# Transposed tiles of a hybrid RWKV-7/HGRN2 layer, moved as 1 KB or 384 B pieces and ordered by a ScalarE copy

## The chip, the core and the metric

The kernel runs on one core of a Trainium2 chip. The core has a matrix engine (TensorE, PE in the profile), whose weight loads are listed apart as PEld, three engines for element work (VectorE or DVE, ScalarE or ACT, GpSimd or POOL), a sync engine (SyncE or SP) that here issues nearly all DMAs, and 16 DMA engines. Each engine works through its own list of instructions in order and waits on semaphores of the others. The metric is device microseconds for one execution of the whole layer, the median of several.

## What is computed

One layer over 512 frames of 2048 channels. A combined input projection feeds two mixers of 1024 channels each. The first is RWKV-7 with 16 heads of 64 channels, the second HGRN2 with 8 heads of 128. Their gated outputs go through one output projection, a residual sum and a layer norm.

```python
# RWKV-7, per head, per frame t
sa = einsum('bhij,bhj->bhi', S, a_t)
S = S * w_t + sa[..., None] * b_t + v_t[..., None] * k_t
o_t = einsum('bhij,bhj->bhi', S, r_t)
...
# HGRN2, per head, chunk by chunk
k_dec = k_c * exp(b_last - b)
S = S * exp(b_last)[..., None] + einsum('bshd,bshv->bhdv', k_dec, i_c)
o = einsum('btsh,bshv->bthv', att, i_c) + einsum('bthd,bhdv->bthv', q_c * exp(b), S)
...
y = concat([o_rwkv * silu(z_r), norm(o_hgrn) * silu(z_h)]) @ W_out
h = layer_norm(ALPHA * h + y)
```

## The kernel before

**The projections.** All projection matmuls are made of three products of split operands: a tile is split into a rounded part (`xh`, `wh`) and the rest (`xl`, `wl`), both in a reduced fp32 format, and `three` (L457) adds hi*hi, hi*lo and lo*hi. A unit of 128 output channels takes 16 channel tiles of the input, so 48 matmuls of 128x512 in one bank of PSUM. The first three units are made by another loop (L1205). Weights arrive as `wr` tiles by DMA; ScalarE makes `wh` (L342), VectorE makes `wl` (L352). The units follow one another in the order of `_order`: for each group of two RWKV channel pairs p the keys k, r and v, the gates z of the group before, then q, f, i and g of the HGRN heads. PSUM has 8 banks, 4 called `main` (projection units and some mixer products) and 4 called `mix`.

**The mixers.** Their work runs beside the projections. RWKV is prepared pair by pair (`rwkv_prep`), then two pairs make a group (`rwkv_group`): a triangular inverse, `folded`, a serial scan over 8 chunks of 64 frames (`rwkv_scan`), `outputs` and `rwkv_finish`. HGRN heads go in twos through `hgrn_heads` and then one by one through `hgrn_out`. In the profile, L329 is a mixer matmul, L333 a transpose by TensorE, L342 and L343 ScalarE activations, L352 a VectorE tensor_tensor, L361 a scalar_tensor_tensor (it also evacuates a projection unit, `t<-main,pr,t`), L371 the VectorE transpose of 32x32 blocks, L310 a DMA that SyncE issues.

**What sets the order.** The kernel is written out instruction by instruction by a planner (`Plan`) that keeps an estimated clock for each engine. Each projection matmul is followed by `pump`, which lets the waiting threads (generators) issue what can start now by those clocks. So the cost that a thread's operation is given decides where everything behind it lands in all engines' lists; on the chip the lists are fixed, and only semaphores hold an engine. The planner knows three kinds of TensorE work (`main`, `whole`, `narrow`), with a cost for each change between them. It puts off mixer matmuls until some are together.

**Buffers.** A thread takes a tile when its pool (`BUFS`) has a free slot by the planner's account and drops it after its last use. A projection unit's bank is emptied into a `t` tile, of which there are 18. When they are short, units wait in their banks (`evac_room`).

**The transposes in question.** Three kinds of tile are transposed with channels and frames changing places: `bk` (beta and k of RWKV, 128x1024 for one pair), v (128x512, written to rows 64 to 127 of the tile `zz`), and k of HGRN heads 0 to 5 (128x384, the first three tiles of 128 frames). VectorE transposes 32x32 blocks (`dtr`) into a `tmp` tile; the blocks then have to change places across partitions, which DMAs do (`turned`): for each of 4x4 (or 4x2) pairs of blocks one DMA of 32 partitions. In each partition such a DMA moves 8 (or 3) runs of 32 floats, 128 B each, straight to the places where matmuls read them. Heads 6 and 7 use TensorE instead.

Of the kernel before, what the change touches and what calls it, by code (L numbers as in the profile page):

```python
# [15 lines left out]
P = 128  # L16
# [225 lines left out]
def mixer_kernel(ctx, tc, head, x_r, w_all, par, up, ln_wb, consts, hmask, out):  # L242
# [127 lines left out]
    def dtr(o, i):  # L370
        return dve_op([i], o, lambda: dve.transpose(o, i), per=0.0019)  # L371
# [22 lines left out]
            f = lambda: dve.tensor_copy(o, i)  # L394
        return Op([act_way(o, i, AF.Copy, scale), ("dve", 0.075 + size(o) * 0.00105 + moved(o, i), f)], [i], [o])

    def turned(dst, src, tmp, rows=4, base=0):


        name = dst.tensor.name  # L400
        yield dtr(tmp, src)
        yield lambda: by_now(tmp)
        for a in range(4):
            for b in range(rows):
                yield lambda: plan.clock["sp"] <= plan.clock["pe"] + 0.2
                o = base + 32 * b
                send(dst[o : o + 32, :, 32 * a : 32 * a + 32],
                     tmp[32 * a : 32 * a + 32, :, 32 * b : 32 * b + 32], 0.65)
        plan.ready[name] = plan.busy[tmp.tensor.name] = (plan.clock["sp"] + 2.6, "dma")

# [213 lines left out]
            ups.append(upw)  # L624

    hc = [slice(64 * h, 64 * h + 64) for h in range(2)]

    def rwkv_prep(S, p):
        if p == 0:
# [71 lines left out]
        drop(pf)  # L701
        yield stt(r, r, hcol(HRK, p), k, ALU.mult, ALU.mult)
        drop(k)
        S["ar"], S["bk"] = ar, bk

        odd = p % 2
        if odd == 0:
# [16 lines left out]

        yield room(q4=1)
        tmp = take("q4", [P, NCH, P])
        yield from turned(bk, bk, tmp)
        drop(tmp)
        yield has(S, "v")
        yield room(ksq=2)  # L730
        rh, rl = (take("ksq", [P, T], F32R) for _ in range(2))
# [9 lines left out]
        S["bv"] = r  # L741

        yield room(zz=1)
        z = take("zz", [P, NCH, P])
        yield room(ksq=1)
        tmp = take("ksq")
        yield from turned(z, chunks(v), chunks(tmp), rows=2, base=64)
        drop(v, tmp)
        S["zz"] = z

    def folded(SS, sc):

        yield lambda: all("zz" in S for S in SS)
        zs, bks = ([S[n] for S in SS] for n in ("zz", "bk"))
        yield room(main=2, mix=2)
        yield landed(*zs, *bks, sc)
        pvs = [take("main") for _ in SS]
        pbs = [take("mix") for _ in SS]
        for half, (z, bk, pv, pb) in enumerate(zip(zs, bks, pvs, pbs)):
            for c in range(NCH):  # L760
                i, cs = half * 16 + 2 * c, slice(c * C, c * C + C)
                for h in range(2):
                    yield mm(pv[hc[h], cs], sc[64:128, 0, i + h], z[64:128, c, hc[h]])
                    yield mm(pb[hc[1 - h], cs], sc[0:64, 0, i + 1 - h], bk[0:64, c, hc[1 - h]])
        more = plan.free("mix", 2)
        prs = []

        def beside():
            prs.extend(take("mix") for _ in SS)
            for half, pr_ in enumerate(prs):  # L770
                for c in range(NCH):
                    for h in range(2):
                        i = half * 16 + 2 * c + h
                        yield mm(pr_[hc[h], c * C : c * C + C], sc[0:64, 0, i], sc[0:64, 1, i])

        if more:
            yield from beside()
        for pv, z, pb, bk in zip(pvs, zs, pbs, bks):
            for h in range(2):
                yield copy(bk[0:64, :, hc[h]], chunks(pb[hc[h]]))  # L780
                yield copy(z[0:64, :, hc[h]], chunks(pv[hc[h]]), scale=-1.0)
# [12 lines left out]
        yield from keep()  # L794

    def outputs(SS, sc):

        yield room(mix=2)
        pss = [take("mix") for _ in SS]
        for half, (S, po) in enumerate(zip(SS, pss)):  # L800
            z = S["zz"]
            yield lambda z=z: by_now(z)
            for c in range(0, NCH, 2):
                for h in range(2):
                    for e in range(2):
                        yield mm(po[hc[e], c // 2 * P + 64 * h : c // 2 * P + 64 * h + 64],
                                 sc[:, 1, half * 16 + 2 * (c + e) + h], z[:, c + e, hc[h]])
# [45 lines left out]
    def rwkv_scan(SS, sc):  # L853
# [15 lines left out]
        olds = [None] * 2  # L869
        for c in range(NCH):  # L870
            more = c < NCH - 1
            zs = [zz[:, c] for zz in zzs]
            news = [bds[c % 2] for bds in bdss]
            pxs = []
            if c > 0:
                yield landed(*olds)
                yield room(mix=2)
                for ar, old in zip(ars, olds):
                    pxs.append(take("mix"))
                    yield mm(pxs[-1][:, :P], ar[:, c], old)  # L880
                for px, z in zip(pxs, zs):
                    yield tt(z[0:64], z[0:64], px[0:64, :P], ALU.subtract)
# [181 lines left out]
    def hgrn_out(S, h, q, k, dt_, dg, tot, tots):  # L1064

        yield room(g=1)
        g = take("g")
        kt, state = tiles(g)[:, 0:3], tiles(k)[:, 0:3]
        if h < 6:
            yield room(ksq=1)  # L1070
            tmp = take("ksq")
            yield from turned(kt, tiles(k)[:, 0:3], tiles(tmp)[:, 0:3])
            drop(tmp)
        else:
            yield landed(k)
# [6 lines left out]
        yield room(rs=1)  # L1082
        i_all = S["i"]
        hs = slice(h % 4 * P, h % 4 * P + P)
        yield landed(i_all, g)
        ps = take("mix")
        for t in range(3):
            yield mm(ps[:, t * P : t * P + P], kt[:, t], i_all[:, t, hs])
# [591 lines left out]
```

## Time and profile before

| what | us |
|---|---|
| median of 3 runs (lowest, highest) | 1052.14 (1050.43, 1052.18) |
| the profiled execution | 1049.71 |
| its span, first to last instruction | 1047.9 |
| ScalarE busy in the span | 436.8 |
| VectorE busy in the span | 754.5 |
| GpSimd busy in the span | 41.8 |

The granted TensorE clock was 0.999 over the span. The profiled execution took 1.8 us more than its span. An instruction's row gives its start, its busy time and, in brackets, the idle time of its engine before it and what ended that. TensorE matmuls are pipelined: their busy times overlap and their ends are modelled, so what a matmul costs is read from one start to the next. "main<-xh,wh" reads: bank `main`, written from tiles `xh` and `wh`.

### The profile page before, as it was taken

The numbers are of one execution on the slowest core, as the hardware profiler recorded it, in microseconds if no ns is written. First come the engines' busy times: TensorE is split into PE (matmuls) and PEld (weight loads), VectorE is DVE, ScalarE is ACT, GpSimd is POOL, SyncE is SP. The second block draws the span as 40 slices with busy tenths as digits, with TensorE's granted clock in tenths as the row PEclk, the third lists the DMA queues.
The fourth block names the chain that finished last, engine by engine and source line by source line (L and its number), as shares of the span: only waits on it lengthen the run. The fifth ranks groups of instructions, "written<-read, shape, count | busy, mean of one in ns | idle before, by whom it ended". The sixth has DMA issues, their size and how long they took to land.

```text
span 1047.9 us, 19640 instructions
## 1 busy us (share of the span) xinstructions
PE 1034.7 (99%) x7708; PEld 857.5 (82%) x7708; DVE 754.5 (72%) x1599; ACT 436.8 (42%) x817; POOL 41.8 (4%) x77
## 2 busy tenths in 40 slices
PE   9999999999999999999999999999999999999997
PEld 7888888888888888878888788888888888888885
DVE  7474898767759988667689767775999886526456
ACT  6444434543443355353533364435335444223321
POOL 0000001001000010010000100100001011000000
PEclk9999999999999999999999999999999999999999
DMA  9135342133253432224443222344342245445613
GB/s 332 53 103 130 90 104 85 60 93 99 77 140 94 123 87 68 87 74 113 112 116 104 82 73 73 105 110 106 105 117 81 64 157 183 145 129 170 193 60 131
DMA packets 98061, 116.03 MB, mean 111 GB/s; under 512 B 67120, under 2 KB 68912, under 8 KB 97840
## 3 DMA queue, kind: packets, MB, share of 16 engines
q1 hardware_dynamic: 97824, 114.57, 37.1%
q8 instruction: 61, 1.00, 0.4%
q14 instruction: 32, 0.26, 0.1%
q10 hardware_dynamic: 144, 0.20, 0.1%
HBM read 99.92 MB, written 7.34 MB: 102 GB/s over the span
## 4 chain that ended last, share of the span: by engine, by line
PE 93%; DMA 2%; DVE 2%; SPq 1%; issue 1%; ACT 0%; POOL 0%; DVEq 0%
PE main L457 70%; PE mix L329 11%; PE mix L457 8%; PE main L1205 3%; DMA wr<-w_all 2%; PE main L329 1%; PE mix L333 1%; SPq L310 1%; DMA q<-head 0%; DVE t L352 0%; DVE wl L352 0%; DVE inv L361 0%; DMA g<-ksq 0%; ACT t L342 0%; DVE q L361 0%
## 5 line engine op out<-in xcount | busy, mean ns | idle before, releaser
L457 PE MATMUL main<-xh,wh 128*128 128x512 f32 x864 | 339.6, 393 | 1.9 <-DVE t L361 1.9
L457 PE MATMUL main<-xh,wl 128*128 128x512 f32 x864 | 341.2, 395 | 0.0
L457 PE MATMUL main<-xl,wh 128*128 128x512 f32 x864 | 339.7, 393 | 0.0
L342 ACT ACTIVATE wh<-wr 128x512 fp32r<-128x512 f32 x299 | 186.5, 627 | 244.7 <-PE main L457 193.6
L352 DVE TENSOR_TENSOR wl<-wr,wh 128x512 fp32r<-128x512 f32 x299 | 203.3, 682 | 75.1 <-ACT wh L342 73.6
L457 PEld LDWEIGHTS main<-xh,wh 128*128 128x128 f32 x864 | 162.4, 188 | 35.3 <-DVE t L361 2.3
L457 PEld LDWEIGHTS main<-xh,wl 128*128 128x128 f32 x864 | 162.4, 188 | 33.3 <-DVE wl L352 0.3
L457 PEld LDWEIGHTS main<-xl,wh 128*128 128x128 f32 x864 | 162.3, 188 | 33.2
L457 PE MATMUL main<-wl,xh 128*128 128x512 f32 (+1 forms) x262 | 102.2, 390 | 0.3 <-DVE wl L352 0.3
L457 PE MATMUL main<-wh,xh 128*128 128x512 f32 (+1 forms) x262 | 102.1, 390 | 0.0
L457 PE MATMUL main<-wh,xl 128*128 128x512 f32 (+1 forms) x262 | 101.8, 388 | 0.0
L457 PEld LDWEIGHTS main<-wl,xh 128*128 128x128 f32 x262 | 49.2, 188 | 10.3 <-DVE wl L352 0.6
L457 PEld LDWEIGHTS main<-wh,xh 128*128 128x128 f32 x262 | 49.2, 188 | 10.2 <-ACT wh L342 0.2
L457 PEld LDWEIGHTS main<-wh,xl 128*128 128x128 f32 x262 | 49.2, 188 | 9.8
L361 DVE SCALAR_TENSOR_TENSOR bd<-mix,pc,bd 64x64 f32<-64x64 f32 x112 | 31.7, 283 | 17.1 <-PE mix L329 15.0
L343 ACT ACTIVATE t<-main,om 128x512 f32<-128x512 f32 x33 | 22.2, 686 | 51.6 <-PE main L457 42.4
L342 ACT ACTIVATE t<-mix 64x128 f32<-64x128 f32 (+2 forms) x65 | 17.6, 272 | 56.6 <-PE mix L329 28.2
L352 DVE TENSOR_TENSOR inv<-inv 64x30 f32<-64x30 f32 (+14 forms) x120 | 38.5, 321 | 2.8
L352 DVE TENSOR_TENSOR inv<-inv,inv 64x30 f32<-64x30 f32 (+14 forms) x120 | 38.5, 321 | 2.7
L361 DVE SCALAR_TENSOR_TENSOR t<-main,pr,t 128x511 f32<-128x511 f32 x33 | 24.3, 745 | 19.7 <-ACT t L343 19.6
L352 DVE TENSOR_TENSOR t<-t,tot 128x256 f32<-128x256 f32 x96 | 37.5, 417 | 0.3
L343 ACT ACTIVATE t<-main 128x512 f32<-128x512 f32 x32 | 18.6, 595 | 32.5 <-PE main L457 32.3
(218 smaller groups left out, 1311.9 us busy)
## 6 DMA issues: line engine op xcount, KB each, us to landing
wr<-w_all SPq DMA_DIRECT2D x156, 512.0 KB, 3.7
q<-head SPq DMA_DIRECT2D x15, 448.0 KB, 6.1
q<-q SPq DMA_DIRECT2D x128, 32.0 KB, 2.7
g<-x_r SPq DMA_DIRECT2D x16, 256.0 KB, 4.0
spill<-g SPq DMA_DIRECT2D x12, 256.0 KB, 3.7
t<-spill SPq DMA_DIRECT2D x12, 256.0 KB, 4.3
out<-q SPq DMA_DIRECT2D x12, 256.0 KB, 2.5
zz<-ksq SPq DMA_DIRECT2D x64, 32.0 KB, 3.0
```

The costliest lines, as they stand in the source:

```text
L310: nc.sync.dma_start(o, i)
L329: return Op([("pe", cost, lambda: pe.matmul(o, l, r, start=start, stop=stop, **kw))], [l, r], [o], mode="narrow" if narrow else "main" if ...
L333: return Op([("pe", 0.11, lambda: pe.transpose(o, i, ident))], [i], [o])
L342: return "act", cost, lambda: sc_e.activation(o, i, f, scale=scale)
L343: return "act", cost, lambda: sc_e.activation(o, i, f, scale=scale, bias=bias)
L352: return dve_op([a, b], o, lambda: dve.tensor_tensor(o, a, b, f), base=0.16 if o.shape[0] < P and size(o) == C and o.tensor.name in tags e ...
L361: return dve_op([a, b], o, lambda: dve.scalar_tensor_tensor(o, a, s, b, f1, f2), per=0.00113, base=0.085 if o.shape[0] == P else 0.25 if s ...
L457: pe.matmul(ps, l, r, start=first and i == 0, stop=last and i == 2)
L1205: pe.matmul(pss[a], *ops, start=k == 0 and low == of == 0, stop=k == KT - 1 and low == 1)
```

## The change

The DMAs of `turned` stay as many as before, and each moves as many bytes. But now the block transpose of VectorE writes its blocks so that what one DMA moves lies together in each partition (`tmp` is indexed block row first, then chunk). The DMA writes to a place where it lies together too: one run of 1 KB (384 B for HGRN keys) in each of 32 partitions. The destination of the DMAs is the source tile itself for `bk` and v, and the head's `g` tile for HGRN keys. A ScalarE copy then puts the blocks into order: `bk` into `tmp`, which takes the name `bk` from there on (8 copies of 128x1024); v into rows 64 to 127 of `zz` (two copies of 64x512 for each of 8 pairs); HGRN keys from `g` back into the k tile (6 copies of 128x384). `zz` is now laid out as four blocks of 32 channels, each with all 8 chunks, so the matmuls that read one chunk of it take two or four runs of 32 floats at a stride of 1 KB, and the VectorE operations that write it do likewise. The planner is told 0.5 us for the issue of one piece, before 0.65 us.

```diff
-    def turned(dst, src, tmp, rows=4, base=0):
-        name = dst.tensor.name
-        yield dtr(tmp, src)
+    def blocks(t, n):
+        return t.rearrange("p (a c j) -> p a c j", a=4, c=n)
+
+    def turned(dst, src, tmp, rows=4):
+        yield dtr(tmp.rearrange("p b c j -> p c b j"), src)
         yield lambda: by_now(tmp)
         for a in range(4):
             for b in range(rows):
                 yield lambda: plan.clock["sp"] <= plan.clock["pe"] + 0.2
-                o = base + 32 * b
-                send(dst[o : o + 32, :, 32 * a : 32 * a + 32],
-                     tmp[32 * a : 32 * a + 32, :, 32 * b : 32 * b + 32], 0.65)
-        plan.ready[name] = plan.busy[tmp.tensor.name] = (plan.clock["sp"] + 2.6, "dma")
+                o = dst(a, b)
+                send(o, tmp[32 * a : 32 * a + 32, b], 0.5)
+        plan.ready[o.tensor.name] = plan.busy[tmp.tensor.name] = (plan.clock["sp"] + 2.6, "dma")
...
         tmp = take("q4", [P, NCH, P])
-        yield from turned(bk, bk, tmp)
-        drop(tmp)
+        bk4 = blocks(bk.rearrange("p c f -> p (c f)"), NCH)
+        yield from turned(lambda a, b: bk4[32 * b : 32 * b + 32, a], bk, blocks(tmp.rearrange("p c f -> p (c f)"), NCH))
+        yield act(tmp.rearrange("p c (a j) -> p c a j", j=32), bk4.rearrange("p a c j -> p c a j"), AF.Copy)
+        drop(bk)
+        S["bk"] = tmp
...
-        z = take("zz", [P, NCH, P])
+        z = take("zz", [P, 4, NCH, 32])
         yield room(ksq=1)
-        tmp = take("ksq")
-        yield from turned(z, chunks(v), chunks(tmp), rows=2, base=64)
-        drop(v, tmp)
+        tmp = take("ksq", [P, 2, NCH, 32])
+        v4 = v.rearrange("p (a c j) -> p a c j", a=2, c=NCH)
+        yield from turned(lambda a, b: v4[64 * (a // 2) + 32 * b : 64 * (a // 2) + 32 * b + 32, a % 2],
+                          chunks(v), tmp, rows=2)
+        drop(tmp)
+        for h in range(2):
+            yield act(z[64:128, hb[h]], v4[hc[h]], AF.Copy)
+        drop(v)
...
-                    yield mm(pv[hc[h], cs], sc[64:128, 0, i + h], z[64:128, c, hc[h]])
+                    yield mm(pv[hc[h], cs], sc[64:128, 0, i + h], z[64:128, hb[h], c])
...
-            zs = [zz[:, c] for zz in zzs]
+            zs = [zz[:, :, c] for zz in zzs]
...
-        kt, state = tiles(g)[:, 0:3], tiles(k)[:, 0:3]
+        kt = state = tiles(k)[:, 0:3]
         if h < 6:
             yield room(ksq=1)
             tmp = take("ksq")
-            yield from turned(kt, tiles(k)[:, 0:3], tiles(tmp)[:, 0:3])
+            g4 = blocks(g[:, : 3 * P], 3)
+            yield from turned(lambda a, b: g4[32 * b : 32 * b + 32, a], kt, blocks(tmp[:, : 3 * P], 3))
             drop(tmp)
+            yield act(kt.rearrange("p c (a j) -> p c a j", j=32), g4.rearrange("p a c j -> p c a j"), AF.Copy)
...
-        yield landed(i_all, g)
+        yield landed(i_all, k)
```

Since the planner's clocks change, the lists of all engines change too. TensorE has the same matmuls as before, in 135 stretches of mixer work between projection matmuls where there were 138. Three places matter below; the number behind a tile's name only tells tiles apart.

The first place is TensorE's list around the output of HGRN head 2 (`mix_4825` before, `mix_4822` now) and the border between two projection units, the gate z of pair 2 (`main_4752`, now `main_4773`) and the key of pair 5 (`main_4866`, now `main_4891`). Before, the border comes 11 projection matmuls behind the head's last product:

```order
L329 MATMUL mix_4825<-t_3494,t_3389 128x128
L457 MATMUL main_4752<-xl_96,wh_4786 128x512
L457 MATMUL main_4752<-xh_80,wl_4787 128x512
...
L457 MATMUL main_4752<-xl_99,wh_4786 128x512
L457 MATMUL main_4752<-xh_83,wl_4787 128x512
L457 MATMUL main_4866<-xh_68,wh_4816 128x512
```

Now it comes 24 projection matmuls and the head's four TensorE transposes behind it:

```order
L329 MATMUL mix_4822<-t_3511,t_3399 128x128
L459 MATMUL main_4773<-xh_76,wh_4786 128x512
L459 MATMUL main_4773<-xl_92,wh_4786 128x512
...
L459 MATMUL main_4773<-xh_82,wl_4787 128x512
L333 MATMUL mix_4868<-cst,t_3399 128x128 x4
L459 MATMUL main_4773<-xh_83,wh_4813 128x512
L459 MATMUL main_4773<-xl_99,wh_4813 128x512
L459 MATMUL main_4773<-xh_83,wl_4814 128x512
L459 MATMUL main_4891<-xh_68,wh_4845 128x512
```

The head's output moved ahead by 13 projection matmuls against the unit border.

The second place is VectorE's list there, where the head's scaled output (`t<-mix,rs`) and the evacuation of the key of pair 4 (`main_4212`, now `main_4234`) stand. Before:

```order
L365 TENSOR_REDUCE rs_4837<-t_3389 128x4
L358 TENSOR_SCALAR rs_4837<-rs_4837 128x4
L352 TENSOR_TENSOR wl_4846<-wr_4703,wh_4845 128x512
L352 TENSOR_TENSOR t_3389<-mix_4825,rs_4837 128x512
L361 SCALAR_TENSOR_TENSOR t_4859<-main_4212,pr,t_4859 128x511
```

Now:

```order
L365 TENSOR_REDUCE rs_4835<-t_3399 128x4
L358 TENSOR_SCALAR rs_4835<-rs_4835 128x4
L352 TENSOR_TENSOR wl_4846<-wr_4769,wh_4845 128x512
L352 TENSOR_TENSOR t_3399<-mix_4822,rs_4835 128x512
L361 SCALAR_TENSOR_TENSOR t_4856<-main_4234,pr,t_4856 128x511
```

Here nothing moved: the evacuation still stands directly behind the head's scaled output.

The third place is ScalarE's list at HGRN head 0, where one of the new copies stands. Now:

```order
L342 ACTIVATE wh_2399<-wr_2288 128x512
L342 ACTIVATE t_1047<-g_2263 128x384
L342 ACTIVATE wh_2419<-wr_2288 128x512
L342 ACTIVATE t_1047<-mix_2432 128x128
L342 ACTIVATE bd_2118<-bd_2119,pc_627 128x128
```

The copy `t_1047<-g_2263` is new; behind it on ScalarE stand a weight split, the head's first state (which before stood there without the copy), and a decay of the scan's state.

More of the change, by code (lines that the diff above doesn't have):

```diff
@@ L626, in mixer_kernel, with halves @@
     hc = [slice(64 * h, 64 * h + 64) for h in range(2)]
+    hb = [slice(2 * h, 2 * h + 2) for h in range(2)]
+    def halves(t):
+        return t.rearrange("p (c a j) -> p c a j", a=2, j=32)
     def rwkv_prep(S, p):
@@ L703, in rwkv_prep @@
         drop(k)
-        S["ar"], S["bk"] = ar, bk
+        S["ar"] = ar
         odd = p % 2
@@ L780, in folded @@
                 yield copy(bk[0:64, :, hc[h]], chunks(pb[hc[h]]))
-                yield copy(z[0:64, :, hc[h]], chunks(pv[hc[h]]), scale=-1.0)
+                yield copy(z[0:64, hb[h]].rearrange("p a c j -> p c a j"), halves(pv[hc[h]]), scale=-1.0)
             drop(pv, pb)
@@ L806, in outputs @@
                         yield mm(po[hc[e], c // 2 * P + 64 * h : c // 2 * P + 64 * h + 64],
-                                 sc[:, 1, half * 16 + 2 * (c + e) + h], z[:, c + e, hc[h]])
+                                 sc[:, 1, half * 16 + 2 * (c + e) + h], z[:, hb[h], c + e])
         for S, po in zip(SS, pss):
@@ L881, in rwkv_scan @@
                 for px, z in zip(pxs, zs):
-                    yield tt(z[0:64], z[0:64], px[0:64, :P], ALU.subtract)
+                    yield tt(z[0:64], z[0:64], px[0:64, :P].rearrange("p (a j) -> p a j", j=32), ALU.subtract)
                 if more:
```

## The prediction

> **What bounds the kernel now.** I read the page's first table, then who TensorE (PE) waited for, then the timeline at each of those waits.
>
> ```profile
> span 1047.9 us, 19640 instructions
> PE 1034.7 (99%) x7708; PEld 857.5 (82%) x7708; DVE 754.5 (72%) x1599; ACT 436.8 (42%) x817; POOL 41.8 (4%) x77
> ```
>
> TensorE is busy in 99% of the span; ScalarE (ACT) and VectorE (DVE) are not. So a transfer or a copy can change the time only where TensorE stands still for it, or where the change gives TensorE more or slower work. All its waits fit in seven lines (total us, times, longest):
>
> ```profile
> PE main L457 <- DVE t L361: 1.9, 1, 1.9
> PE mix L329 <- ACT ksq L1422: 1.5, 1, 1.5
> PE mix L329 <- issue: 1.3, 3, 0.8
> PE main L329 <- issue: 1.3, 1, 1.3
> PE mix L1155 <- DVE inv L1153: 1.1, 1, 1.1
> PE mix L329 <- DMA g<-ksq: 0.6, 1, 0.6
> PE main L457 <- DVE wl L352: 0.3, 1, 0.3
> ```
>
> They add up to 8.0 us, 0.8% of the span: no removal of waits can bring more. Only one of them, `g<-ksq`, is a wait for a DMA that the change touches. The waits on ksq L1422 and inv L1153 are at the end and the start of the kernel, where nothing changes. What the change does to the other lines it does by moving work.
>
> **The largest wait, for a bank.** First TensorE, then VectorE, at 455 to 460 us; the columns are start, busy time, instruction.
>
> ```profile
> 455.13 0.39 PE L329 MATMUL mix<-t,t 128*128 128x128 f32 x2
> 455.27 0.48 PE L457 MATMUL main<-xl,wh 128*128 128x512 f32 x1
> 457.44 0.39 PE L457 MATMUL main<-xl,wh 128*128 128x512 f32 x1
> 457.68 0.39 PE L457 MATMUL main<-xh,wl 128*128 128x512 f32 x1
> 459.98 0.50 PE L457 MATMUL main<-xh,wh 128*128 128x512 f32 x1 [1.92 <-DVE t L361]
> ...
> 456.19 0.69 DVE L365 TENSOR_REDUCE rs<-t 128x4 f32<-128x512 f32 x1 [2.12 <-ACT t L343]
> 458.58 0.69 DVE L352 TENSOR_TENSOR t<-mix,rs 128x512 f32<-128x512 f32 x1 [0.90 <-POOL rs L384]
> 459.19 0.74 DVE L361 SCALAR_TENSOR_TENSOR t<-main,pr,t 128x511 f32<-128x511 f32 x1
> ```
>
> Projection matmuls start 0.23 us apart (457.44 to 457.68); here one starts 2.30 us after the one before, so 2.07 us are lost. The key of pair 5 needs the bank of the key of pair 4, four units older, whose evacuation ends at 459.19 + 0.74 = 459.93. That evacuation stands behind HGRN head 2 on VectorE: reduce, GpSimd's reciprocal root, scaled output. The head's last product starts at 455.13, so the bank comes free 4.80 us after it. TensorE has only 11 projection matmuls to fill this, and arrives at 459.98 - 2.07 = 457.91.
>
> **Part 1: the order.** The rows of TensorE's order say that 24 projection matmuls and four transposes now lie in this place, while VectorE's rows keep the evacuation directly behind the head. Twenty-four steps of 0.23 us are 5.5 us, more than the 4.80 us that the bank takes. The wait should go: **-2.07 us**, and 0.7 us plus the transposes remain as a margin. What is late next there: the transposes need the scaled output, which ends at 458.58 + 0.69 = 459.27, 4.14 us behind the last product, and they stand 21 steps, 4.8 us, behind it. That fits by 0.7 us. Bounds: 0 to -2.07.
>
> **Part 2: the pieces.** The wait of `g<-ksq` is at HGRN head 0:
>
> ```profile
> 257.39 0.39 PE L457 MATMUL main<-xl,wh 128*128 128x512 f32 x1
> 258.33 0.91 PE L329 MATMUL mix<-ia,g 128*128 128x128 f32 x6 [0.56 <-DMA g<-ksq]
> ...
> 253.16 1.87 SPq L310 DMA_DIRECT2D g<-ksq  x3
> ...
> q<-q SPq DMA_DIRECT2D x128, 32.0 KB, 2.7
> zz<-ksq SPq DMA_DIRECT2D x64, 32.0 KB, 3.0
> g<-ksq SPq DMA_DIRECT2D x96, 12.0 KB, 2.2
> out<-inv SPq DMA_DIRECT2D x2, 128.0 KB, 3.1
> ```
>
> The product starts 0.94 us after the matmul before it where 0.23 is usual: 0.71 us lost. Three pieces took 1.87 us of the sync engine's time, 0.62 each, and the last was issued at about 254.4. The planner counted 0.65 a piece and now counts 0.5. What a piece of 32 runs takes there isn't in the trace; the nearest row is the weight load of 128 partitions, 0.33:
>
> ```profile
> 256.92 0.33 SPq L310 DMA_DIRECT2D wr<-w_all  x1
> ```
>
> Between 0.33 and 0.62 I take 0.33, since a new piece has fewer runs than that load. Sixteen pieces are then done 16 x (0.5 - 0.33) = 2.7 us before the planner counts on them, where before the gain was 16 x (0.65 - 0.62) = 0.5 us. This wait should go: **-0.71 us**, bounds 0 to -0.71.
>
> How soon a piece lands would matter as well. Pieces in runs of 128 B land in 2.2 to 3.0 us, a store of 128 KB in long rows in 3.1: short runs cost little here. The Trainium skill, "DMA: Bandwidth & Descriptors", section "Why small descriptors are slow (HBM only)", says that transfers within SBUF don't suffer from small descriptors as those to HBM do; the rows agree. It speaks against this part: if transport is all that the change shortens, the 0.71 us stay and the sum below ends 0.7 us higher. I keep the term, because it comes from the issue, 0.62 us a piece, and not from the landing.
>
> **Part 3: the added copies.** No row shows them; these are the nearest:
>
> ```profile
> L342 ACT ACTIVATE wh<-wr 128x512 fp32r<-128x512 f32 x299 | 186.5, 627 | 244.7 <-PE main L457 193.6 <-PE mix L457 32.9 <-DMA wr<-w_all 6.9
> L342 ACT ACTIVATE q<-mix 64x512 f32<-64x512 f32 x16 | 9.5, 593 | 8.1 <-PE mix L329 8.0
> L342 ACT ACTIVATE t<-q 128x384 fp32r<-128x384 f32 x15 | 7.6, 510 | 1.4 <-DMA q<-head 1.4
> ```
>
> Eight copies of 1024 at twice 0.63 are 10.1 us, 16 of 64x512 at 0.59 are 9.5, 6 of 384 at 0.51 are 3.1: **22.7 us** on ScalarE, whose 436.8 us busy leave 611 us idle. As work they lie beside TensorE and cost nothing; the cover is that ScalarE's splits (`wh`) run ahead until a buffer holds them, as their 193.6 us of waiting for projection matmuls show. The price is the new wait: each copy waits on ScalarE for DMA pieces, and behind it in the list stand weight splits and evacuations, as in the third place of the order. VectorE needs `wh` for `wl`, TensorE needs both, and the sync engine's next weight load waits for `wl`. If a copy waits longer than the splits are ahead, TensorE stands. Bounds: 0, and 22 groups (8 `bk`, 8 v, 6 k) each late by as much as the one wait on pieces above, 22 x 0.71 = 15.6 us. Since one group in 22 was late before, I take one again: **+0.7 us**. So parts 2 and 3 cancel; they are kept apart because they can fail apart.
>
> **Part 4: the rest of TensorE's work.** The matmuls are the same. Three fewer returns from mixer work to projections save little: one return shows above, 455.13 to 455.27 and then 0.32 to the next start instead of 0.23. With 0.1 to 0.15 us each that is **-0.4 us** (0 to -0.5). Short runs in the moving operand `zz` could cost time. One group of matmuls reads a moving operand in runs before too (the first row, HGRN levels that take every other stretch of 2 to 16 floats); the others read `zz`, so far in one run:
>
> ```profile
> L329 PE MATMUL mix<-t,t 128*32 128x16 f32 x512 | 6.2, 185 | 0.2 <-issue 0.2
> L329 PE MATMUL mix<-zz,q 128*128 128x128 f32 x112 | 17.2, 275 | 0.0
> L329 PE MATMUL main<-zz,big 64*64 64x64 f32 x256 | 10.0, 221 | 1.3 <-issue 1.3
> L329 PE MATMUL mix<-zz,big 128*64 128x64 f32 x256 | 8.3, 224 | 0.0
> ```
>
> By busy time the first takes 6.2 / 512 = 12 ns for 16 columns, 0.75 ns each. The `zz` rows take 154 ns for 128 (1.2 each), 39 ns for 64 (0.61) and 32 ns for 64 (0.51). So runs far shorter than 32 floats cost at most 0.75 ns a column. I take 0 for the new layout; the upper bound raises the last two rows to 0.75 ns, 48 ns each, which is 256 x (9 + 16) ns = 6.4 us.
>
> The 2.6 us of "issue" fall inside unbroken bursts of small matmuls, the longest here, where no row shows anything that it waited for:
>
> ```profile
> 186.17 0.22 PE L329 MATMUL mix<-q,big 64*64 64x64 f32 x1
> 187.67 0.27 PE L329 MATMUL main<-zz,big 64*64 64x64 f32 x1 [1.28 <-issue]
> ```
>
> Such bursts stay: the planner now cuts this one in two and lengthens others. Bounds -2.6 to +2.6 (all gone, or twice as many); I take 0.
>
> VectorE's transposes and its sums into `zz` keep their number and size and write runs of 128 B; nothing on TensorE waited for them, so I take 0 there too.
>
> **The sum.** The profiled execution took 1049.71 us, its span and 1.8 us around it. -2.07 - 0.71 + 0.7 - 0.4 = -2.5 gives 1047.2. The median of the runs shown is 1052.14, 2.4 us above that execution, so the forecast for a median is 1047.2 + 2.4 = **1049.6 us**. This is 0.24% below, hardly more than the 0.2% that a measurement of this kernel can tell from no change.
>
> **Rivals.**
>
> *The waits come back elsewhere.* Every list is new, and the planner's errors that made the 2.07 us (a bank counted free 2 us too early) are still in it. For it: units still queue in their banks, as the unchanged VectorE rows show. Against it: in a thousand microseconds only one such wait came. One more of 2.07 us gives 1049.6 + 2.1 = 1051.7, no change.
>
> *The copies hold up the splits.* This is the case that ends slower. The place is ScalarE's list behind each copy. It decides from the point where pieces land later than the splits are ahead; a wait of 0.71 us at half of the 22 groups is +7.8 us, less the one already counted: 1049.6 + 7.1 = 1056.7. For it: weight loads stand between the pieces on the sync engine and can hold them; from 249 to 257 us, around the late pieces of head 0, the sync engine's waits had this one line:
>
> ```profile
> SPq L310 <- DVE wl L352: 1.8, 1, 1.8
> ```
>
> Against it: only 0.3 us of TensorE's waiting was for `wl`, and the planner issues a copy only when it counts the pieces as landed, with the 2.7 us of margin of part 2.
>
> *The matmuls read `zz` slower*: 1049.6 + 6.4 = 1056.0, by the bound of part 4. For it speaks only that no row shows this layout; against it, that much shorter runs come within that bound already.
>
> *The change does not act.* The bank's wait stays, since the planner's list says nothing on when VectorE gets there: 1051.7 as well.
>
> **How the numbers follow.** The forecast has 0.55: within it, 0.44 falls over 0.2% below and 0.11 short of that. That waits come back or stay has 0.32, all within 0.2%. The copies as a brake have 0.10 and the slow reading of `zz` 0.03. So faster 0.44, same 0.43, slower 0.13. The range reaches down to 1045.5, where the waits in the bursts would go too (1049.6 - 2.6 = 1047.0, and 1.5 us less since runs of the kernel before lie 1.7 us apart), and up to 1054.5, some two thirds of the way to the brake's time. The two ends leave out some 0.07 below and 0.12 above.
>
> **What would show it.** Right: no wait of PE main L457 on DVE t L361 near 455 us, no wait of `mix<-ia,t` on pieces, pieces at about 0.33 us of the sync engine, ACT busy up by some 23 us, and a PE wait list of some 5 to 6 us. Wrong: PE waiting on `wl` or `wh` behind a copy, `mix<-zz,q` above its mean of 275 ns, or a new bank wait of 2 us elsewhere.

## The result and the profile after

The changed kernel takes 1052.98 us in the median of 12 runs (1051.28 to 1056.09); the kernel before takes 1050.44 in 12 runs beside it (1049.07 to 1052.18). The ratio is 1.0027, with a 95% interval of 1.0015 to 1.0039. It is slower by 2.5 us, where the forecast had it faster by as much. The profiled execution took 1055.96 us, 1054.2 of them span, at a mean granted clock of 0.995 (before 0.999). It is one of the three longest of the twelve: a stretch at half clock (the last section shows it) makes it longer than most, so below the waits of the two profiles are compared, not their spans.

The page's first table after, and then TensorE's waits (engine and line, what it waited for: total us, times, longest):

```profile
span 1054.2 us, 19704 instructions
PE 1040.1 (99%) x7708; PEld 859.9 (82%) x7708; DVE 752.3 (71%) x1600; ACT 456.6 (43%) x847; POOL 44.6 (4%) x77
...
PE mix L329 <- DVE ksq L352: 2.9, 6, 1.3
PE mix L329 <- issue: 2.5, 3, 1.8
...
PE mix L329 <- ACT ksq L342: 0.9, 2, 0.6
```

The bank wait and the wait for pieces of `g` are gone. In their place stand the two `ksq` lines, eight waits: the products of `ksq` with a matrix of ones, for which r*k is split into `rh` (ScalarE, L342) and `rl` (VectorE, L352). Where they come from is seen in ScalarE's waits for pieces:

```profile
ACT q L342 <- DMA q<-q: 25.5, 8, 5.7
ACT zz L342 <- DMA t<-ksq: 11.4, 8, 2.2
ACT t L342 <- DMA g<-ksq: 10.9, 5, 3.7
```

The copies made ScalarE stand for 47.8 us in 21 waits, and every copy of `bk` waited. One of them, at pair 6: SyncE, then ScalarE, VectorE and TensorE, each row with start, busy time and, in brackets, the idle time before it.

```profile
690.68 7.00 SPq L310 DMA_DIRECT2D q<-q  x10
697.78 0.53 SPq L310 DMA_DIRECT2D wr<-w_all  x1
698.41 3.68 SPq L310 DMA_DIRECT2D q<-q  x6
...
703.59 1.06 ACT L342 ACTIVATE q<-q 128x1024 f32<-128x1024 f32 x1 [3.50 <-DMA q<-q]
704.56 0.61 ACT L342 ACTIVATE ksq<-t 128x512 fp32r<-128x512 f32 x1
...
705.20 0.69 DVE L352 TENSOR_TENSOR ksq<-t,ksq 128x512 fp32r<-128x512 f32 x1 [3.91 <-ACT ksq L342]
...
704.27 0.39 PE L459 MATMUL main<-xh,wh 128*128 128x512 f32 x1
705.22 0.50 PE L329 MATMUL mix<-ksq,ones_r 128*128 128x512 f32 x1 [0.56 <-ACT ksq L342]
705.95 0.50 PE L329 MATMUL mix<-ksq,ones_r 128*128 128x512 f32 x1 [0.23 <-DVE ksq L352]
```

Sixteen pieces with a weight load between them take SyncE from 690.68 to 702.09, 11.4 us where the planner counts 16 x 0.5 = 8. The copy stands on ScalarE for 3.50 us; directly behind it stands the split `rh`, behind that on VectorE `rl`, behind that TensorE. The first product starts 0.95 us after the matmul before it, the second 0.73 after the first, where 0.23 is usual: 1.2 us lost. Over all pairs the products of `ksq` lose 5.65 us, from start to start: 0.5 to 1.4 us in each of six of the eight pairs, nothing in the other two.

### The profile page after: what moved, and what is told of

Read it like the earlier page. It is cut to its first block, busy times and chain, and to the rows that moved or that the text cites. A ratio compares the mean times of both kernels' runs of the same rounds, so it can differ in the third digit from the quotient of the medians.

```text
span 1054.2 us, 19704 instructions
## 1 busy us (share of the span) xinstructions
PE 1040.1 (99%) x7708; PEld 859.9 (82%) x7708; DVE 752.3 (71%) x1600; ACT 456.6 (43%) x847; POOL 44.6 (4%) x77
## 4 chain that ended last, share of the span: by engine, by line
PE 90%; DVE 5%; DMA 2%; issue 1%; SPq 1%; ACT 1%; ACTq 0%; DVEq 0%
PE main L459 66%; PE mix L329 10%; PE mix L459 8%; PE main L1221 3%; DVE inv L352 1%; PE main L329 1%; DMA q<-q 1%; SPq L310 1%; DVE wl L352 1%; PE mix L333 1%; DVE t L352 1%; PE mix L1171 0%; DVE ksq L352 0%; DVE inv L361 0%; DMA t<-ksq 0%
## 5 line engine op out<-in xcount | busy, mean ns | idle before, releaser
L342 ACT ACTIVATE wh<-wr 128x512 fp32r<-128x512 f32 x299 | 186.2, 626 | 220.7 <-PE main L459 173.0
L352 DVE TENSOR_TENSOR wl<-wr,wh 128x512 fp32r<-128x512 f32 x299 | 203.7, 682 | 77.4 <-ACT wh L342 76.0
L361 DVE SCALAR_TENSOR_TENSOR bd<-mix,pc,bd 64x64 f32<-64x64 f32 x112 | 31.7, 283 | 18.8 <-PE mix L329 16.9
L352 DVE TENSOR_TENSOR inv<-inv,inv 64x30 f32<-64x30 f32 (+14 forms) x120 | 38.5, 321 | 2.8
L352 DVE TENSOR_TENSOR inv<-inv 64x30 f32<-64x30 f32 (+14 forms) x120 | 38.5, 320 | 2.6
L352 DVE TENSOR_TENSOR t<-t,tot 128x256 f32<-128x256 f32 x96 | 37.9, 417 | 0.3
L342 ACT ACTIVATE t<-mix 64x128 f32<-64x128 f32 (+3 forms) x70 | 19.2, 277 | 41.6 <-DVE zz L352 27.0
```

The source lines that it names most:

```text
L342: return "act", cost, lambda: sc_e.activation(o, i, f, scale=scale)
L352: return dve_op([a, b], o, lambda: dve.tensor_tensor(o, a, b, f), base=0.16 if o.shape[0] < P and size(o) == C and o.tensor.name in tags e ...
L361: return dve_op([a, b], o, lambda: dve.scalar_tensor_tensor(o, a, s, b, f1, f2), per=0.00113, base=0.085 if o.shape[0] == P else 0.25 if s ...
```

## The experiments

Three theories. **A**: the copies cost, by waiting on ScalarE for their pieces while splits and evacuations stand behind them. **B**: the new lists cost, whatever is moved; the planner's list is another one and has other accidents. **C**, added on the way: the pieces, the layout or the copies' work cost by themselves, whoever waits. Each ratio below is to the kernel before on the same chip, with its 95% interval. No run leaves out a part of the computation.

### Changing the planner's input

**The copy of `bk` written behind the split of r*k**, in the changed kernel:

```diff
-        yield act(tmp.rearrange("p c (a j) -> p c a j", j=32), bk4.rearrange("p a c j -> p c a j"), AF.Copy)
-        drop(bk)
-        S["bk"] = tmp
         yield has(S, "v")
...
+        yield act(tmp.rearrange("p c (a j) -> p c a j", j=32), bk4.rearrange("p a c j -> p c a j"), AF.Copy)
+        drop(bk)
+        S["bk"] = tmp
```

> The changed kernel with the ScalarE copy of bk written behind the split of r*k (rh, rl) in the same thread, no longer ahead of it. Theory A (the copy waits on ScalarE for its pieces, and the split behind it makes TensorE wait for ksq): the lines PE mix L329 <- DVE ksq L352 and <- ACT ksq L342, 3.8 us together in the changed kernel, fall below 0.5 us, and the time falls by 3 to 5.5 us against the changed kernel, to a ratio of 0.995 to 1.000 with the kernel before. Theory B (every new list of instructions costs or gains a few us by chance): the ksq lines may go but waits of the same size appear elsewhere, ratio 1.000 to 1.005.

**The changed kernel with 0.6 us counted for a piece:**

```diff
-                send(o, tmp[32 * a : 32 * a + 32, b], 0.5)
+                send(o, tmp[32 * a : 32 * a + 32, b], 0.6)
```

> The changed kernel with 0.6 us instead of 0.5 counted by the planner for the issue of one piece (a piece takes 0.58 in the trace). Theory A with the count as the cause: the copies of bk stand 16 x 0.1 = 1.6 us later in ScalarE's list, so ScalarE's wait for q<-q falls from 25.5 us (8 times 3.2) by about 12 us, the ksq lines fall from 3.8 to under 1.5 us, and the time falls by 2 to 5 us against the changed kernel. If the count is not the cause but the landing or the weight loads between the pieces: the waits stay above 20 us and 2.5 us. Theory B: ratio 0.998 to 1.005 without a link to the ksq lines.

**The kernel before with 0.60, and with 0.70, counted for a piece.** Nothing but the lists changes:

```diff
-                     tmp[32 * a : 32 * a + 32, :, 32 * b : 32 * b + 32], 0.65)
+                     tmp[32 * a : 32 * a + 32, :, 32 * b : 32 * b + 32], 0.6)
```

> The kernel before with 0.60 instead of 0.65 counted for one piece: no instruction differs, only the planner's lists. It shows how much a new list alone is worth. Theory A: within 0.15% of the kernel before (1.5 us). Theory B: it can move by 0.2 to 0.4% either way; the wait of 2 us for the bank of the key of pair 4 comes or goes with it.

> The kernel before with 0.70 instead of 0.65 counted for one piece, a second new list with no other change. If the list of the kernel before is an especially good one (as the count of 0.60, ratio 1.0036, suggests): 1.002 to 1.010. If the count of 0.60 was bad because it is too small (a piece takes 0.61): within 0.15%.

| run | median us | ratio |
|---|---|---|
| split ahead of the copy | 1067.86 | 1.0176 (1.0157 to 1.0196) |
| changed kernel, 0.6 | 1066.86 | 1.0172 (1.0154 to 1.0191) |
| before, 0.60 | 1053.09 | 1.0036 (1.0021 to 1.0052) |
| before, 0.70 | 1048.77 | 1.0000 (0.9988 to 1.0011) |

In the first run the `ksq` lines of after are gone, as theory A has it, and yet it is slower by 1.8%. The second run has the largest wait of all, on TensorE:

```profile
476.57 1.08 PE L333 MATMUL mix<-cst,t 128*128 128x128 f32 x4 [7.79 <-DVE t L352]
```

That has nothing to do with a piece or a copy: the transposes of HGRN head 2 had come right to the border of a unit. Theory B is true as far as it goes. In the third run nothing but the list is new, and it costs 0.36%; 0.05 us in the planner's count of a piece was enough. (The 1.8% of the first two are list and transport together.) So a run whose lists are free tells nothing on the copies, and the first two failed as tests. The next runs hold the lists still.

### Lists and transport apart

**The lists of the kernel before, with the change's pieces, layout and 30 copies.** The planner doesn't know of the copies; each is put into ScalarE's list when the planner counts its pieces as landed, less 0.6 us. All other engines keep their lists word for word.

```diff
+        plan.pending.append((plan.ready[nt][0] - 0.6, "q4", lambda tmp=tmp, bk4=bk4: sc_e.activation(
+            tmp.rearrange("p c (a j) -> p c a j", j=32), bk4.rearrange("p a c j -> p c a j"), AF.Copy, scale=1.0)))
```

> The change's pieces, layout and copies in the lists of the kernel before: TensorE, VectorE, GpSimd and SyncE have the same instructions in the same order as before, ScalarE has the 30 copies added, each about where the planner counts its pieces as landed (so behind the split of r*k). Against the kernel before it shows the moves and copies alone. Theory A (the moves and copies cost time on the chip): ratio 1.002 to 1.006, with TensorE waiting 3 us or more behind copies. Theory B (the loss is in the new lists): within 0.15% of the kernel before, the bank wait of 1.9 us on DVE t L361 still there, no ksq lines.

**The lists of the changed kernel with the transport of the kernel before.** The planner counts the copies, but none is issued, since the 128 B runs land in place:

```diff
+    def counted(n, narrow, i, o):
+        return Op([("act", 0.09 + n * 0.00085 + (0.1 if narrow else 0.0), lambda: None)], [i], [o])
...
-        yield act(tmp.rearrange("p c (a j) -> p c a j", j=32), bk4.rearrange("p a c j -> p c a j"), AF.Copy)
+        yield counted(1024, False, bk, tmp)
```

> The lists of the changed kernel with the transport of the kernel before: 128 B runs straight to their places, no ScalarE copies (the planner counts them, nothing is issued); all other instructions in the changed kernel's order. Theory A: the ksq waits are gone, 3 to 6 us faster than the changed kernel, ratio 0.996 to 1.000 with the kernel before, since the bank wait is gone as well. Theory B: within 1.5 us of the changed kernel, ratio 1.001 to 1.004.

| ratio | transport before | transport of the change |
|---|---|---|
| lists before | 1 | 1.0051 (1.0032 to 1.0070) |
| lists of the change | 0.9989 (0.9977 to 1.0002) | 1.0027 (1.0015 to 1.0039) |

The transport costs 0.4 to 0.5% in either lists; the new lists by themselves cost nothing and may gain 0.1%. For this change theory B falls. In the old lists the ratio is what theory A expected, but TensorE's waits behind copies are 2.1 us where it expected 3 or more, and the bank wait of 1.9 us is still there, as it must be with those lists. With the old transport in the new lists, TensorE waits for no piece and for no `ksq` behind a copy. Its longest line of waits names nothing ("issue"), and the next, 1.5 us, is at the end of the kernel:

```profile
PE mix L334 <- issue: 2.8, 4, 2.0
```

**One part of the change in the kernel before, lists free:** only `bk`, and only v and the HGRN keys.

> Of the change only the bk part: 1 KB pieces and a ScalarE copy for bk, v and the HGRN keys as before. Theory A: the ksq lines are there with 3 to 5 us, and the time is 0.2 to 0.5% above the kernel before. If the copies of v or of the keys make the loss, or theory B holds: ksq lines under 1 us or a time within 0.15% of the kernel before.

> Of the change only the parts of v and the HGRN keys; bk as before, with 0.65 counted for its pieces. Theory A (the bk copy ahead of the split of r*k): no ksq lines. Its list is new as well; from the three new lists so far (ratios 1.0036 to 1.0176) a ratio of 1.002 to 1.018 by theory B, 0.997 to 1.001 by theory A.

They gave 1.0072 (1.0055 to 1.0089) and 1.0082 (1.0062 to 1.0101). Each is slower than both together, so each has its own accidents of lists, and both ratios lie above what theory A expected. But the waits are of its kind: in the first TensorE waits for `ksq` behind copies of `bk`, in the second for the copy of HGRN keys itself (`t`, L342), 4.6 us in two waits.

```profile
PE mix L329 <- ACT ksq L342: 3.1, 2, 2.1
PE mix L329 <- DVE ksq L352: 1.7, 3, 1.3
```

### One part at a time in the lists before

In these four all engines but ScalarE have the lists of the kernel before, and ScalarE's list differs by the copies alone. The first puts the copies 1.5 us later by the planner's clock (`+ 0.9` in place of `- 0.6` above).

> The lists of the kernel before on TensorE, VectorE, GpSimd and SyncE, with the pieces, the layout and the 30 copies of the change, as in the fourth experiment; but each copy is put into ScalarE's list 1.5 us later by the planner's clock, so that its pieces have landed when ScalarE gets there. Theory A (the cost is that copies wait on ScalarE for their pieces, and splits and evacuations behind them are late): ScalarE's waits for pieces fall from 34.4 us to under 12 us, TensorE's waits on ScalarE behind copies go, and the ratio falls from 1.0051 to 1.000 to 1.002. Theory C (the cost is in the copies' work, the pieces or the layout themselves, whoever waits): the ratio stays at 1.004 to 1.006 although the waits for pieces go. A copy that comes too late for its reader would show as TensorE waiting on a copy itself.

> The lists of the kernel before on all engines, plus only the 8 copies of bk and its 1 KB pieces; v and the HGRN keys move as before and zz keeps its layout. Theory A: of the 34.4 us that the copies waited in the fourth experiment 15.6 were bk's, so about half of its loss: 1.002 to 1.003, the rest in the run with v and the keys alone. Theory B (lists alone; moves cost nothing): 1.000. Rival that the layout of zz costs the time: 1.000 here as well.

> The lists of the kernel before on all engines, no copies, every transposed tile moved in 128 B runs as before, but zz has the change's layout of four blocks of 32 channels, so TensorE reads it and VectorE writes it in runs of 128 B. Theory A: 1.000 (within 0.2%), mix<-zz,q at 275 ns. Rival that the layout costs the time: 1.003 to 1.006.

> The lists of the kernel before on all engines, with the change's pieces, layout and 22 copies of v and of the HGRN keys; bk moves as before. Theory A: the part of the fourth experiment's loss that bk does not explain, 1.002 to 1.003, with ScalarE waiting some 19 us for pieces of v and keys. If the two parts add up, this ratio and that of bk alone give 1.0051 together.

| run, lists before | median us | ratio |
|---|---|---|
| all parts, copies 1.5 us later | 1055.52 | 1.0056 (1.0041 to 1.0071) |
| `bk` alone | 1054.28 | 1.0054 (1.0033 to 1.0074) |
| layout of `zz` alone | 1050.09 | 1.0005 (0.9994 to 1.0016) |
| v and keys with the layout | 1051.48 | 1.0017 (1.0004 to 1.0030) |

The first missed what theory A expected. Its ScalarE waits for pieces (in the run with the early copies they were 15.6, 11.4 and 7.4 us):

```profile
ACT q L753 <- DMA q<-q: 13.1, 6, 4.0
ACT t L1111 <- DMA g<-ksq: 3.7, 3, 1.3
ACT zz L779 <- DMA t<-ksq: 2.9, 2, 2.3
```

The waits for v and keys fell from 18.8 us to 6.6, those for `bk` only from 15.6 to 13.1, and the time did not move. So the waits of v and keys cost little, and `bk`'s were not tested. `bk` alone costs as much as all, twice what theory A expected of it; v and keys cost a third of it; the layout costs nothing that can be told from zero, as expected. The two parts add up to 1.0071 where all together gave 1.0051, which the intervals allow.

What one waiting copy does is read from the profile of `bk` alone, against the kernel before, since the lists are the same. At 763 us, before and then with the copy, ScalarE, then VectorE's list some 35 us on, then TensorE:

```profile
761.14 0.63 ACT L342 ACTIVATE wh<-wr 128x512 fp32r<-128x512 f32 x1 [1.89 <-PE main L457]
...
763.30 0.67 DVE L352 TENSOR_TENSOR wl<-wr,wh 128x512 fp32r<-128x512 f32 x1
...
794.29 0.54 DVE L358 TENSOR_SCALAR t<-t,lw 128x512 f32<-128x512 f32 x1
...
798.22 0.89 PE L329 MATMUL mix<-q,t 128*32 128x48 f32 x64
```

```profile
763.07 1.06 ACT L752 ACTIVATE q<-q 128x1024 f32<-128x1024 f32 x1 [3.58 <-DMA q<-q]
764.04 1.13 ACT L353 ACTIVATE wh<-wr 128x512 fp32r<-128x512 f32 x2
...
764.69 0.69 DVE L363 TENSOR_TENSOR wl<-wr,wh 128x512 fp32r<-128x512 f32 x1 [1.04 <-ACT wh L353]
...
795.38 1.30 DVE L369 TENSOR_SCALAR t<-t,lw 128x512 f32<-128x512 f32 x1
...
795.45 0.94 POOL L398 MEMSET big<- 32x1024 f32 x1 [42.90 <-PE mix L340]
...
798.57 0.55 PE L340 MATMUL mix<-q,t 128*32 128x48 f32 x32
800.41 0.55 PE L340 MATMUL mix<-q,t 128*32 128x48 f32 x32 [1.29 <-ACT q L353]
801.48 0.63 PE L468 MATMUL main<-xl,wh 128*128 128x512 f32 x1
801.91 0.63 PE L468 MATMUL main<-xh,wl 128*128 128x512 f32 x1
```

The copy waits 3.58 us. The weight split behind it, at 761.14 before, starts at 764.04, and VectorE waits 1.04 us for it in the middle of a triangular inverse that leaves it hardly any idle time. It comes out of it 1.09 us later than before, at 795.38 (0.28 us of that the run had behind it already), just as GpSimd begins its memsets; beside them the operation takes 1.30 us instead of 0.54; that they slow it is argued from the overlap alone. The scan's operand is late, and at 800.41, 37 us behind the copy, TensorE waits 1.29 us. The matmuls after that start 0.43 us apart instead of 0.23, because the clock was granted at one half for the next 3.4 us. The columns here are the stretch, its length, busy time and count by engine, then the clock:

```profile
800.90:804.30 3.40, 3.40 (x18) 2.27 (x15) 2.88 (x9) 1.65 (x4) 0.00 (x0) 0.50 0.51 159
```

So a wait of 1.3 us was paid with 1.7 us more, half of the 3.4. TensorE's lag behind the kernel before grows from 0.3 to 3.4 us at this place. The median of this run lies 4.6 us above that of the kernel before; where the rest is lost isn't traced. The Trainium skill, "TensorE: Matmul & The Clock Gate", section "What's actually happening", has the clock fall to one half after an idle window of about 3.4 us. The length of the dip agrees with that window; the idle time does not, since the dip here followed a wait of 1.29 us. That this wait alone started it isn't shown.

### The copies of `bk` put later, lists still

**`bk` alone in the lists before**, with `+ 6.0` in place of `- 0.6`; and **the changed kernel** with the copy's issue put off, after the planner has counted it where it did:

```diff
+    def later(op, tag):
+        (e, cost, f), = op.ways
+        op.ways = [(e, cost, lambda: plan.pending.append((plan.clock["pe"] + 5.0, tag, f)))]
+        return op
...
-        yield act(tmp.rearrange("p c (a j) -> p c a j", j=32), bk4.rearrange("p a c j -> p c a j"), AF.Copy)
+        yield later(act(tmp.rearrange("p c (a j) -> p c a j", j=32), bk4.rearrange("p a c j -> p c a j"), AF.Copy), "q4")
```

> The run with bk alone in the lists of the kernel before, with its copies 6.6 us later by the planner's clock where no buffer forbids it, which puts them 2 to 6 places further back in ScalarE's list, behind the weight splits that they held up; nothing else moves. Theory A (the cost is the copy's wait on ScalarE): ScalarE's waits for pieces of bk fall from 13.5 us to under 5 us, TensorE's wait on q<-t near 800 us (1.3 us) goes, and the ratio falls from 1.0054 to 1.000 to 1.002. Theory C (the cost is in the copies' work or the pieces): the ratio stays at 1.004 to 1.006.

> The changed kernel with its lists on TensorE, VectorE, GpSimd and SyncE; on ScalarE seven of the 8 copies of bk stand 3 to 6 places further back, behind the split of r*k and the weight splits, the eighth stays. Theory A: TensorE's 5.7 us at the products of ksq with ones_r go almost wholly, and the ratio falls from 1.0027 to 0.998 to 0.9995, about that of the new lists without copies (0.9989). Theory C: it stays at 1.002 to 1.004.

| run | median us | ratio |
|---|---|---|
| lists before, `bk` alone, copies later | 1052.09 | 1.0026 (1.0013 to 1.0038) |
| changed kernel, `bk`'s copies later | 1046.73 | 0.9984 (0.9968 to 1.0000) |

In the first, ScalarE's wait for pieces of `bk` fell from 13.5 us to 2.3, the wait at 800 us is gone, and half of the loss with it, 1.0054 to 1.0026, where theory A expected at most 1.002. The other half is not explained by a wait on a copy: its list of TensorE's waits has none. What grew in that profile are waits that name nothing, 5.1 us against 2.6 before. They vary from run to run, so this rest stays open, and for the lists before theory C is not excluded.

The second decides for the changed kernel. By the two traces seven of the eight copies stand 2 to 5 places further back on ScalarE, and every other list is the changed kernel's own. TensorE's waits, and then pair 6, which above lost 1.2 us, on ScalarE and TensorE:

```profile
PE mix L340 <- issue: 2.0, 2, 1.5
...
PE mix L340 <- DVE ksq L363: 1.3, 1, 1.3
...
697.32 0.61 ACT L353 ACTIVATE ksq<-t 128x512 fp32r<-128x512 f32 x1
701.23 1.06 ACT L353 ACTIVATE q<-q 128x1024 f32<-128x1024 f32 x1 [0.97 <-DMA q<-q]
...
701.59 0.40 PE L475 MATMUL main<-xh,wh 128*128 128x512 f32 x1
701.82 0.64 PE L340 MATMUL mix<-ksq,ones_r 128*128 128x512 f32 x2
702.30 0.40 PE L475 MATMUL main<-xl,wh 128*128 128x512 f32 x1
```

The split of r*k now comes ahead of the copy, and TensorE runs through. The one `ksq` wait behind a copy that is left, 1.3 us, is that of pair 1, whose copy could not be moved. The ratio goes from 1.0027 to 0.9984: 0.43%, or 4.5 us, with some 2 us of uncertainty either way by the two intervals.

The profiles say the same without the medians. TensorE's list is the same in both, so one matmul can be looked up in each, first in the changed kernel, then with the copies later:

```profile
799.17 0.89 PE L329 MATMUL mix<-q,t 128*32 128x48 f32 x64
```

```profile
794.66 0.89 PE L340 MATMUL mix<-q,t 128*32 128x48 f32 x64
```

At 799 us the version with later copies is 4.51 us ahead. Of the eight steps of more than 0.3 us by which its lead changed from one matmul to the next until then, seven are at products of `ksq`; the eighth goes the other way. (Behind this place the changed kernel's profile has its stretch at half clock, which this comparison leaves out.)

This version is faster than the changed kernel, and against the kernel before its interval just reaches 1. It is not told apart from the same lists with the old transport (0.9989), so the larger pieces bring nothing even when the copies do no harm.

## Why the prediction was wrong

**Part 1, the order: right.** The bank wait of 2.07 us is gone, as the rows of the order said. In the changed kernel VectorE's evacuation frees the bank at 456.26 + 0.74 = 457.00, and TensorE comes to the border 1.35 us later without a wait:

```profile
456.26 0.74 DVE L361 SCALAR_TENSOR_TENSOR t<-main,pr,t 128x511 f32<-128x511 f32 x1
...
458.35 0.40 PE L459 MATMUL main<-xh,wh 128*128 128x512 f32 x1
```

The new lists with the old transport show what all of it was worth: 0.11% of 1049 us, 1.2 us, with an interval from 2.4 us gained to 0.2 lost. The forecast had 2.07 + 0.4 for the lists, which is at the end of that interval; where the rest went isn't shown.

**Part 2, the pieces: the wait went, but not for the reason given.** `g<-ksq` is gone from TensorE's list; it is gone with the old transport in the new lists too, so the lists removed it. That it went as forecast is luck. The piece was taken at 0.33 us of SyncE, from a weight load that stands alone; the load behind a piece, 4 us before it in the same list, took 0.53. Here are that load, three pieces of `bk` in the changed kernel, and what pieces take there from issue to landing (the last column, median us):

```profile
252.59 0.53 SPq L310 DMA_DIRECT2D wr<-w_all  x1
```

```profile
141.19 1.77 SPq L310 DMA_DIRECT2D q<-q  x3
...
q<-q SPq DMA_DIRECT2D x128, 32.0 KB, 2.3
t<-ksq SPq DMA_DIRECT2D x64, 32.0 KB, 2.6
g<-ksq SPq DMA_DIRECT2D x96, 12.0 KB, 1.9
```

That is 0.59 us a piece, near the 0.62 of the old ones, where 0.33 was taken; the sixteen of pair 6 above took 7.00 + 3.68 = 10.68 us, 0.67 each. Landing fell by 0.3 to 0.4 us, so the short runs had cost that little. The planner counts 0.5, so sixteen pieces are not 2.7 us early but 16 x 0.09 = 1.4 us late, 2.7 at pair 6, before any weight load comes between them.

**Part 3, the copies: this step failed.** Their work was sized well, 21.7 us of ScalarE against 22.7. Their price was put at 0.7 us and is 4.5 us for `bk` in the changed kernel's lists. Two things in it were wrong. It counted one late group of 22, because one was late before, where every copy of `bk` waited and six of the eight pairs lost time, since the margin it leaned on was the 2.7 us of part 2. (That 0.71 us a group came near the mark is luck: 5.65 us over eight pairs is 0.7 each, but a pair loses from 0 to 1.4.) And it named weight splits and evacuations as what stands behind a copy, and counted on the splits to run ahead. In the changed kernel's list the split of r*k stands directly behind seven of the copies of `bk`, one place further behind the eighth, and pair 6 shows no cover: it ends on ScalarE at 705.17, and TensorE starts its product at 705.22. Nor did weight splits always have cover: in the lists before, a late one at 764 us led to the wait at 800. The rival "the copies hold up the splits" was the right mechanism, and "slower" had a chance of 0.13. Its price was off: 7.1 us above the forecast, for half of 22 groups, where in this list `bk`'s eight do it and v and keys cost nothing that can be told from zero. The sign that the prediction named for it, TensorE waiting on `wl` or `wh` behind a copy, did not come up; the waits were on `ksq`.

**Part 4: right.** The layout of `zz` costs nothing that can be told from zero, 1.0005, and its 112 matmuls stay at 275 ns in the run that changes the layout alone (281 in the changed kernel's profile, where four of them lie in the stretch at half clock and took 416 to 422):

```profile
L329 PE MATMUL mix<-zz,q 128*128 128x128 f32 x112 | 17.2, 275 | 0.0
```

The waits that name nothing were 2.6 us before and 2.5 after. The rival "the matmuls read `zz` slower" falls; "the change does not act" falls by part 1.

**The sum.** Lists -1.2 us, the place of `bk`'s copies +4.5, and the rest of the transport -0.5, which is inside its interval, make +2.8, where the forecast had -2.5. The three are steps between four ratios, so they add up to 1.0027 by construction and are no test of it; between the medians it is 2.5 us. The forecast also started from a median of three runs, 1052.14, where twelve gave 1050.44.

## What to carry to other kernels

A copy that waits for a DMA costs what stands behind it in its engine's list, not its own time: before adding one, name the next instructions there, ask which of them has cover, and put the copy behind those that have none. Fewer and larger runs in a DMA help only if something waits for the transfer itself; the issue of 0.6 us a piece stayed, and it set when the last piece came. And where a planner writes the lists, a change of one cost moves the time by as much as the change under test, so hold the lists still and change one thing in them.

## What the runs showed of the hardware

**SyncE's issue hardly follows the number of runs.** Eight pieces of `bk` at the same place of the same list, in the kernel before (256 runs of 128 B each) and with `bk` alone changed (32 runs of 1 KB each):

```profile
747.37 5.17 SPq L310 DMA_DIRECT2D q<-q  x8
```

```profile
747.65 5.00 SPq L321 DMA_DIRECT2D q<-q  x8
```

That is 0.65 us a piece and 0.63. The number of rows does not set it alone either: a weight load of 128 partitions took 0.33 us in the prediction's row and 0.53 directly behind a piece (252.59 and 697.78 above). What does set it isn't shown.

**The waits that name nothing lie at borders of the instruction stream.** Counted along TensorE's instructions, with weight loads and its waits on semaphores, 62 of the 63 that the 16 profiles show lie at place 192 or 193 modulo 256, nearly all in or right behind bursts of small matmuls. The instructions themselves arrive in packets of about 16 KB: 60 packets with 0.98 MB in the changed kernel.

The Trainium skill, "Runtime: NRT & Kernel Launch", section "Instruction fetch mechanics", has blocks of 256 instructions, which agrees, and holds the fetch mostly hidden; here TensorE stood 1.79 us at such a border of the changed kernel:

```profile
803.63 0.27 PE L329 MATMUL mix<-q,big 64*64 64x64 f32 x1 [1.79 <-issue]
```

That the fetch is what it waits for is argued from the place alone; no run changed it.

**Half the clock follows some waits.** Behind that wait the changed kernel's profile had a mean clock of 0.57 over 11.8 us:

```profile
803.60:815.40 11.80, 11.77 (x103) 9.76 (x104) 7.00 (x20) 4.59 (x8) 0.00 (x0) 0.57 0.01 2
```

The bank wait of 1.92 us, before, had no such dip. Of the twelve executions of the changed kernel the three with a mean clock of 0.995 or 0.996 took 1055.90 to 1056.09 us, the five at 1.000 took 1051.28 to 1053.67: the same list can cost microseconds more in one execution than in the next.
